# Fourier sums over both halves at once, one Silu, a gate group first, and the context rows moved to the fourth and fifth groups

## The chip, the cores and the metric

The kernel runs on one core of one Trainium2 chip. The metric is the device time of one execution in microseconds. Three timed executions of the kernel before gave 1290.10, 1290.96 and 1291.08 us; the median is 1290.96 us.

## The reference

The reference is one layer of a diffusion block over 512 latent tokens of width 2048, with 256 context tokens. All inputs and outputs are fp32. Cut to what matters here, with `h` the normalised and modulated tokens and `hc` the normalised and modulated context:

```
p   = h @ w_in                       # columns q | k | v | z_a | u_b | z_b | g_a | g_b
q   = rope(rmsnorm(q)) * scale;  k = rope(rmsnorm(k));  kc, vc = hc @ w_in[k | v]
y_a = (attention(q, [k, kc], [v, vc]) * silu(z_a)) @ w_pa
y_b = (real(fft2(u_b over 512 positions and 4 groups of 128 channels)) / 256 * silu(z_b)) @ w_pb
out = rmsnorm(x + gate * ((sigmoid(g_a) * y_a + sigmoid(g_b) * y_b) @ w_out))
```

The Fourier mixing is done as matrix products with tables of cosines and sines. Along the 512 positions, the sums and the differences of the two halves of the tokens give the even and the odd frequencies; along the 128 channels of a group, one table of cosines and one of sines follows. A real input needs 257 frequencies of 512, the others are their mirror images.

## The kernel before

**Arithmetic.** An fp32 matrix is split into a high part, which ACT rounds off (L180), and a low part, which DVE gets by subtraction (L181). A product is then three TensorE passes, high by high (L338), low by high (L339) and high by low (L340); `mm3` issues the three.

**Stages.** The first 144.6 us load the tokens, compute the modulation and project u_b and z_b. The channel stage, to 156.1 us, computes the Fourier mixing: `tokens(g)` (for each of four channel groups) sums over positions into a bank `pb` in two parts, even and odd frequencies, and splits each result into `ah` and `al` (L180, L181); `positions(g)` sums over channels into a bank `pd` (L939, L942), and L944 multiplies the result by 1/256 and by silu(z_b) into `part`; `gate_b(g)` makes silu(z_b) by a Sigmoid on ACT (L949) and a multiplication on DVE (L950).

From 156.1 us on come eight groups of 1024 columns of w_in. Each is seven Strassen products (P1, Q5, P2, Q6, P7, Q3, Q4) of four pieces of 12 matmuls of 512 columns. A product takes 10.9 us, a group 76.2 us: the groups start at 156.1, 234.1, 310.2, 386.4, 463.0 and 539.2 us, and so on. `KINDS` gives their kinds: three "qz" groups (queries and z_a), two "gate" groups, one "kv" group, two "gate" groups. After them come attention, the projection of the branches, and the output.

**What sets the order.** PE runs its instructions in order. Weights come as raw tiles `wr` and `R` by SP's and POOL's queues, are partly summed on DVE (L268, L276), and are split into `whi` and `wlo`, or into `s` where a form of the tokens is split. The instructions of the channel stage on PE stand in the order of the code; elsewhere a scheduler in the framework sets each engine's order when the kernel is built. In the channel stage, splits of the first weight pieces of group 0 are put behind given instructions of `tokens`.

**After a group's product.** A quarter of a "qz" group holds queries: `rotated` (L1208 on ACT, L1210, L1212, L1215, L1216 on DVE, two operations on POOL) normalises and rotates a 128x1024 half of them into the tile `qr`, and two DMAs on ACT's queue (L1230) store it to `qz_d` in device memory. This work of group g runs beside the first products of group g+1. A "gate" half only takes a Sigmoid on ACT (L1183) and a DMA to `g_d`.

**The context.** The tile `qr` has 2048 columns. During the "qz" groups the first 1024 hold the rotated queries and the others the rotary tables. Later the same tile holds the context's forms: `diag` is its first 256 columns, `cparts` its first 1792, `crs` its last 256. Four raw pieces of context ("cn") give the sums of squares; `context_norm` turns them into two diagonal matrices `diag` (L1315, DVE); `context_spread` multiplies `ones` by them on PE (L1320) and copies the result to `crs` (L1321, ACT); four pieces ("cr") then each go through `context_row`, which fills `cparts` and stores it to `cf_d` by a DMA on ACT's queue (L1345). The "kv" group reads `cf_d` back on SP's queue (L216). `context_piece` says beside which weight piece of groups 3 and 4 each is taken, and the list `jobs` holds small tasks, of which one is issued after each piece of a product.

Of the kernel before, what the change touches and what calls it, by code (L numbers as in the profile page):

```python
# [18 lines left out]
P = 128  # L19
D = 2048  # L20
T = 512
# [26 lines left out]
EVEN = 258  # L48
# [16 lines left out]
KINDS = ("qz", "qz", "qz", "gate", "gate", "kv", "gate", "gate")  # L65
# [57 lines left out]
def block_kernel(ctx, tc, xT, ctx_rows, ctx_toks, x, c_row, w_ss, w_gate, vecs, qkg, rope, dft_c, dft_s,  # L123
# [243 lines left out]
    for p in start_pieces():  # L367
        if p[2:5:2] == (KK - 4, 0):
            stream(("dfts", 0), dft_s[:, : 2 * EVEN], 2 * EVEN, 2, "raw")
            stream(("dftc", 0), dft_c, 3 * P, 1, "raw")  # L370
        elif p[2:5:2] == (KK - 4, 4):
            stream(("dfts", 1), dft_s[:, 2 * EVEN :], T, 2, "raw")
        stream(("start", p), w_start[p[0] : p[0] + P * p[1]].rearrange("(p c) -> p c", p=P), p[1], p[2 + 1])
# [146 lines left out]
    fch = ppool.tile([P, 2, 3 * P], F32R, name="fch")  # L520
    fsq = [ppool.tile([P, 2, 2, EVEN], F32R, name="fsq0")]
# [374 lines left out]
    fsq.append(fnp.tile([P, 2, 2, 256], F32R, name="fsq1"))  # L896
# [19 lines left out]
    AH, low = {}, {}  # L916

    def tokens(g):

        ah, al = (fnp.tile([P, 2, 257], F32R, tag=n, bufs=2, name=uid(n)) for n in ("ah", "al"))  # L920
        c = slice(P * g, P * g + P)
        for e in range(2):
            n = fsq[e].shape[-1]
            acc = bank()
            for a in range(2):
                mm3(acc[:, :n], uh[:, a, e, c], ul[:, a, e, c], fsq[e][:, 0, a, :], fsq[e][:, 1, a, :], a == 0, a == 1)
            k = slice(e, 257 - e, 2)
            low[g] = split_from(acc[:, :n].rearrange("p (r f) -> p r f", r=2), ah[:, :, k], al[:, :, k])[1]
        AH[g] = ah, al

    def positions(g):

        ah, al = AH.pop(g)
        acc = bank2()
        steps = [(256 * q, P * (r and 1 + q), (slice(0, 256) if q == 0 else slice(256, 0, -1)), r)
                 for q in range(2) for r in range(2)]
        for n, (o, t, k, r) in enumerate(steps):
            for m, i in enumerate((0, 1)):
                nc.tensor.matmul(acc[:, o : o + 256], fch[:, i, t : t + P], ah[:, r, k], start=n == m == 0, stop=False,  # L939
                                 skip_group_check=True)  # L940
        for n, (o, t, k, r) in enumerate(steps):
            nc.tensor.matmul(acc[:, o : o + 256], fch[:, 0, t : t + P], al[:, r, k], start=False, stop=n == 3,  # L942
                             skip_group_check=True)
        nc.vector.scalar_tensor_tensor(part[:, 4 + g, :], acc, 1.0 / 256.0, part[:, 4 + g, :], op0=ALU.mult, op1=ALU.mult)  # L944

    def gate_b(g):
        z = part[:, 4 + g, :]
        e = fnp.tile([P, T], F32, tag="sil", bufs=1, name=uid("e"))
        nc.scalar.activation(e, z, ACT.Sigmoid)  # L949
        nc.vector.tensor_tensor(z, z, e, op=ALU.mult)  # L950
# [3 lines left out]
    for g in range(4):  # L954
# [265 lines left out]
    def qz_done(half, c, v, t):  # L1220
# [8 lines left out]
        for b in range(2):  # L1229
            nc.scalar.dma_start(qz_d[4 * group.g : 4 * group.g + 4, :, c, 2 * half + b, :].rearrange("h p d -> p h d"),  # L1230
# [73 lines left out]
    def context_squares(i, raw):  # L1304

        nc.scalar.activation(raw, raw, ACT.Square, accum_out=sums[:, i : i + 1])

    def context_norm():

        ss = sums[:, 4:6]  # L1310
        nc.vector.tensor_tensor(ss, sums[:, 0:4:2], sums[:, 1:4:2], op=ALU.add)
# [11 lines left out]
    def context_row(i, raw):  # L1323
# [11 lines left out]
        for j in range(2):  # L1335
            sa, sb = (shift[:, 2 * i + j + 8 * q, 1:2] for q in range(2))
            d = sums[:, 6 + j : 7 + j]
# [731 lines left out]
```

## Time and profile before

| | |
|---|---|
| median of the runs | 1290.96 us |
| the profiled execution's own time | 1290.61 us |
| its span in the profile | 1288.8 us |
| busy share: PE, DVE, ACT, POOL | 99%, 77%, 53%, 13% |
| channel stage, 144.6 to 156.1 us: busy PE, DVE, ACT | 11.50, 11.22, 8.48 us |
| group 0, 156.1 to 234.1 us: busy PE, DVE, ACT | 77.05, 75.57, 42.22 us |
| group 3, 386.4 to 463.0 us: busy PE, DVE, ACT | 76.60, 65.24, 43.44 us |
| mean granted TensorE clock | 0.998 |

The span is the time from the profile's first to its last instruction; 1.8 us of the execution lie outside it. A timeline row has the start, the duration, the engine, the line, the operation and its tiles, and in brackets the idle time before it with what ended that. Matmuls overlap, so that their pitch (start to start) and not their duration says how fast they follow: 0.12 us for 256 or 258 columns, 0.23 us for 512.

### The profile page before, as it was taken

To read this page: it belongs to the slowest core of one execution; us is meant where nothing else is said; L and a number is where in the kernel's file an instruction comes from. 1 tells how busy PE (TensorE), PEld (TensorE's weight loads), DVE (VectorE), ACT (ScalarE), POOL (GpSimd) and SP (SyncE) were. 2 spreads that over 40 slices of the span, in tenths; PEclk is the share of its full clock that TensorE was granted. 3 is DMA by queue.
4 is the path that set the end of the run, shared out by engine and by line. 5 is a ranking of instruction groups with operands and counts; after the bars stand their busy time and mean duration, and the time that the engine had idled before them with its cause. 6 is when DMAs were issued, how large, how long until landed. Compare 5 with 4: busy or idle time off the path is not lost.

```text
span 1288.8 us, 17680 instructions
## 1 busy us (share of the span) xinstructions
PE 1272.9 (99%) x6586; PEld 1047.9 (81%) x6586; DVE 994.7 (77%) x1305; ACT 682.2 (53%) x1073; POOL 170.8 (13%) x222
## 2 busy tenths in 40 slices
PE   8999999999999999999999999999999999999997
PEld 5677887888888888888888888888888888888886
DVE  5767899889779787658587666788898777887677
ACT  5322654645556555444355544666667646464544
POOL 0000011111102011012031010012100211211210
PEclk9999999999999999999999999999999999999999
DMA  9998588888988988977879897578852989998986
GB/s 378 408 369 344 208 216 248 237 218 261 227 302 236 301 269 260 291 197 184 278 207 259 286 249 237 182 245 241 270 178 75 249 244 258 244 211 229 225 200 179
DMA packets 104486, 319.14 MB, mean 248 GB/s; under 512 B 9904, under 2 KB 33072, under 8 KB 100432
## 3 DMA queue, kind: packets, MB, share of 16 engines
q1 hardware_dynamic: 55056, 197.40, 42.3%
q0 software_dynamic: 27024, 98.19, 35.6%
q10 hardware_dynamic: 22320, 22.42, 5.1%
q8 instruction: 51, 0.84, 0.3%
q14 instruction: 35, 0.29, 0.1%
HBM read 283.36 MB, written 34.61 MB: 247 GB/s over the span
## 4 chain that ended last, share of the span: by engine, by line
PE 91%; DVE 3%; DMA 2%; ACT 2%; issue 1%; SPq 0%; ACTq 0%; DVEq 0%
PE banks L338 10%; PE banks L339 10%; PE banks L340 10%; PE x L340 9%; PE x L338 9%; PE x L339 9%; PE y L340 7%; PE y L339 7%; PE y L338 7%; PE banks L1543 2%; PE pd L566 2%; PE pb L338 1%; PE pb L339 1%; PE pb L340 1%; PE pc L338 1%; DMA wa<-in_w_ss 1%
## 5 line engine op out<-in xcount | busy, mean ns | idle before, releaser
L180 ACT ACTIVATE whi<-R 128x1024 fp32r<-128x1024 f32 x138 | 145.6, 1060 | 142.1 <-PE banks L340 55.3
L181 DVE TENSOR_TENSOR wlo<-R,whi 128x1024 fp32r<-128x1024 f32 x138 | 167.9, 1222 | 57.9 <-ACT whi L180 57.6
L181 DVE TENSOR_TENSOR wlo<-wr,whi 128x1024 fp32r<-128x1024 f32 (+1 forms) x122 | 147.2, 1214 | 63.1 <-ACT whi L180 63.1
L180 ACT ACTIVATE whi<-wr 128x1024 fp32r<-128x1024 f32 (+1 forms) x122 | 127.4, 1052 | 127.3 <-PE y L340 44.3
L338 PE MATMUL banks<-whi,s 128*128 128x512 f32 (+1 forms) x400 | 157.8, 394 | 0.9 <-DVE ev L1106 0.9
L339 PE MATMUL banks<-wlo,s 128*128 128x512 f32 (+1 forms) x400 | 155.8, 389 | 0.0
L340 PE MATMUL banks<-whi,s 128*128 128x512 f32 (+1 forms) x400 | 155.8, 389 | 0.0
L338 PE MATMUL x<-whi,s 128*128 128x512 f32 x352 | 137.1, 390 | 0.0
L340 PE MATMUL x<-whi,s 128*128 128x512 f32 x352 | 137.0, 389 | 0.0
L339 PE MATMUL x<-wlo,s 128*128 128x512 f32 x352 | 136.9, 389 | 0.0
L338 PE MATMUL y<-whi,s 128*128 128x512 f32 x316 | 123.1, 389 | 0.2 <-DVE cxe L1266 0.2
L339 PE MATMUL y<-wlo,s 128*128 128x512 f32 x316 | 123.1, 390 | 0.0
L340 PE MATMUL y<-whi,s 128*128 128x512 f32 x316 | 122.8, 389 | 0.0
L291 POOL DMA_DIRECT2D R<-in_w_g x64 | 56.0, 875 | 415.2 <-DVE wlo L181 212.6
L180 ACT ACTIVATE s<-wr 128x512 fp32r<-128x512 f32 (+2 forms) x93 | 60.9, 678 | 68.1 <-DMA wr<-cf_d 24.9
L338 PEld LDWEIGHTS banks<-whi,s 128*128 128x128 f32 x400 | 75.2, 188 | 16.6 <-DVE ev L1106 1.3
L181 DVE TENSOR_TENSOR s<-wr,s 128x512 fp32r<-128x512 f32 (+2 forms) x93 | 66.7, 750 | 28.3 <-ACT s L180 27.5
L340 PEld LDWEIGHTS banks<-whi,s 128*128 128x128 f32 x400 | 75.1, 188 | 15.3
L339 PEld LDWEIGHTS banks<-wlo,s 128*128 128x128 f32 x400 | 75.2, 188 | 13.6 <-DVE wlo L181 0.2
L340 PEld LDWEIGHTS x<-whi,s 128*128 128x128 f32 x352 | 66.1, 188 | 13.8
L339 PEld LDWEIGHTS x<-wlo,s 128*128 128x128 f32 x352 | 66.1, 188 | 13.7
L338 PEld LDWEIGHTS x<-whi,s 128*128 128x128 f32 x352 | 66.1, 188 | 13.6
(322 smaller groups left out, 2803.2 us busy)
## 6 DMA issues: line engine op xcount, KB each, us to landing
wr<-in_w_g SPq DMA_DIRECT2D x128, 512.0 KB, 5.8
R<-in_w_g POOLq DMA_DIRECT2D x64, 512.0 KB, 7.3
wa<-in_w_ss SPq DMA_DIRECT2D x31, 1024.0 KB, 9.7
R<-in_w_g SPq DMA_DIRECT2D x32, 512.0 KB, 6.0
wr<-in_w_gate SPq DMA_DIRECT2D x32, 512.0 KB, 5.1
wr<-in_w_o SPq DMA_DIRECT2D x24, 512.0 KB, 7.5
R<-in_w_o POOLq DMA_DIRECT2D x24, 512.0 KB, 9.2
wr<-in_w_pab SPq DMA_DIRECT2D x20, 512.0 KB, 6.0
```

The costliest lines, as they stand in the source:

```text
L180: first = nc.scalar.activation(hi, src, ACT.Copy)
L181: return first, nc.vector.tensor_tensor(lo, src, hi.bitcast(F32), op=ALU.subtract)
L291: nc.gpsimd.dma_start(chain[e.pc], e.nxt, accum_op=ALU.add)
L338: nc.tensor.matmul(o, ah, bh, start=start, stop=False, skip_group_check=cont)
L339: nc.tensor.matmul(o, ah, bl, start=False, stop=False, skip_group_check=cont)
L340: nc.tensor.matmul(o, al, bh, start=False, stop=stop, skip_group_check=cont)
L566: nc.tensor.matmul(acc[32 * j : 32 * j + 32], c2[:, n, :], w[:, k, :], start=n < 4, stop=n >= KK - 4)
L1543: nc.tensor.transpose(tp[:, k * P : (k + 1) * P], p[:, k * P : (k + 1) * P], ident)
```

## The change

1. In the channel stage the even frequencies become a table of 129 as before, the odd ones too (128 before): both are 258 wide (`FREQ`). `positions` no longer makes the two mirrored halves as separate sums; it computes the cosine sum and the sine sum once for 258 frequencies, in two banks `pd` and `pc`. ACT copies the second into `odd`, and DVE writes the difference (257 columns) and the sum in reversed order (255 columns) to a tile `y`. The factor 1/256 is in the table of channels.
2. `gate_b` is one Silu on ACT. The multiplication of `y` by silu(z_b) stands after the splits of the first weight pieces (L962).
3. The order of the groups is gate, qz, qz, qz, gate, kv, gate, gate; the columns of `w_g` and the index in `qz_d` follow.
4. The pieces of context move: the sums of squares to group 3, pieces 16, 18, 20 and 22 of its 28 (P7 and Q3), the rows to group 4, its pieces 5, 10, 15 and 20. `context_norm` and `context_spread` are appended to the jobs at the start of group 4, with one empty job between them; before, they were appended at the start of group 3 behind twelve empty jobs. Their sums have columns of their own.

```
-KINDS = ("qz", "qz", "qz", "gate", "gate", "kv", "gate", "gate")
+KINDS = ("gate", "qz", "qz", "qz", "gate", "kv", "gate", "gate")
...
+CTX_NORM, CTX_ROWS = (16, 18, 20, 22), (33, 38, 43, 48)
...
-    if n % 2 == 0 and 0 <= n < 8:
-        return "cn", n // 2
-    if n % 7 == 4 and 18 <= n < 46:
-        return "cr", n // 7 - 2
+    if n in CTX_NORM:
+        return "cn", CTX_NORM.index(n)
+    if n in CTX_ROWS:
+        return "cr", CTX_ROWS.index(n)
...
     def positions(g):
 
         ah, al = AH.pop(g)
-        acc = bank2()
-        steps = [(256 * q, P * (r and 1 + q), (slice(0, 256) if q == 0 else slice(256, 0, -1)), r)
-                 for q in range(2) for r in range(2)]
-        for n, (o, t, k, r) in enumerate(steps):
-            for m, i in enumerate((0, 1)):
-                nc.tensor.matmul(acc[:, o : o + 256], fch[:, i, t : t + P], ah[:, r, k], start=n == m == 0, stop=False,
-                                 skip_group_check=True)
-        for n, (o, t, k, r) in enumerate(steps):
-            nc.tensor.matmul(acc[:, o : o + 256], fch[:, 0, t : t + P], al[:, r, k], start=False, stop=n == 3,
-                             skip_group_check=True)
-        nc.vector.scalar_tensor_tensor(part[:, 4 + g, :], acc, 1.0 / 256.0, part[:, 4 + g, :], op0=ALU.mult, op1=ALU.mult)
+        acc = [b()[:, :FREQ] for b in (bank2, bank3)]
+        for r, o in enumerate(acc):
+            t = slice(P * r, P * r + P)
+            mm3(o, fch[:, 0, t], fch[:, 1, t], ah[:, r, :], al[:, r, :], True, True)
+        odd = fnp.tile([P, FREQ], F32, tag="odd", bufs=2, name=uid("odd"))
+        y = mixed[g] = fnp.tile([P, T], F32, tag="y", bufs=4, name=uid("y"))
+        nc.scalar.copy(odd, acc[1])
+        nc.vector.tensor_tensor(y[:, :257], acc[0][:, :257], odd[:, :257], op=ALU.subtract)
+        nc.vector.tensor_tensor(y[:, 257:], acc[0][:, 255:0:-1], odd[:, 255:0:-1], op=ALU.add)
 
     def gate_b(g):
         z = part[:, 4 + g, :]
-        e = fnp.tile([P, T], F32, tag="sil", bufs=1, name=uid("e"))
-        nc.scalar.activation(e, z, ACT.Sigmoid)
-        nc.vector.tensor_tensor(z, z, e, op=ALU.mult)
+        nc.scalar.activation(z, z, ACT.Silu)
...
             for e in ahead[:g]:
                 split_piece(e)
+    for g in range(4):
+        z = part[:, 4 + g, :]
+        nc.vector.tensor_tensor(z, mixed[g], z, op=ALU.mult)
...
-        if g == 3:
-            jobs += [lambda: None] * 12 + [context_norm, lambda: None, lambda: None, context_spread]
+        if g == KV - 1:
+            jobs += [context_norm, lambda: None, context_spread]
```

**What the change moves on the engines.** Lines of the changed kernel are numbered up to three higher (L181 is L184 there, L1216 is L1217, L1315 is L1316, L1320 is L1321, L1230 is L1231).

In the channel stage DVE's order before was this (`al` is a low part of a Fourier sum, `wlo` and `s` those of group 0's weights and tokens, L944 and L950 the multiplications by 1/256 and silu):

```order
L181 TENSOR_TENSOR al_1497<-pb_1498,ah_1496 128x2x129
L950 TENSOR_TENSOR part<-part,e_1578 128x512
L181 TENSOR_TENSOR al_1497<-pb_1507,ah_1496 128x2x128
L181 TENSOR_TENSOR wlo_1575<-R_1340,whi_1574 128x1024
L944 SCALAR_TENSOR_TENSOR part<-pd_1519,part 128x512
L181 TENSOR_TENSOR al_1534<-pb_1535,ah_1533 128x2x129
L181 TENSOR_TENSOR al_1534<-pb_1544,ah_1533 128x2x128
L181 TENSOR_TENSOR wlo_1596<-R_1341,whi_1595 128x1024
L944 SCALAR_TENSOR_TENSOR part<-pd_1560,part 128x512
L268 TENSOR_TENSOR R_1339<-R_1339,wr_1353 128x1024
```

and now is this:

```order
L184 TENSOR_TENSOR al_1528<-pb_1529,ah_1527 128x258
L184 TENSOR_TENSOR wlo_1566<-R_1340,whi_1565 128x1024
L184 TENSOR_TENSOR al_1528<-pb_1538,ah_1527 128x258
L943 TENSOR_TENSOR y_1561<-pd_1552,odd_1560 128x257
L944 TENSOR_TENSOR y_1561<-pd_1552,odd_1560 128x255
L184 TENSOR_TENSOR wlo_1584<-R_1341,whi_1583 128x1024
L943 TENSOR_TENSOR y_1579<-pd_1570,odd_1578 128x257
L944 TENSOR_TENSOR y_1579<-pd_1570,odd_1578 128x255
L962 TENSOR_TENSOR part<-y_1489,part 128x512
L962 TENSOR_TENSOR part<-y_1523,part 128x512
```

The four multiplications by silu(z_b) stand behind the low part of the third weight piece now, and a low part of a weight piece stands between the two last `al`, which the last sum over channels needs.

The spreading of the context's norms on PE stood between the products Q6 and P7 of group 3 (the last rows of Q6 with its bank `y`, the first of P7 with its bank `x`):

```order
L338 MATMUL y_3463<-s_433,s_1869 128x512
L339 MATMUL y_3463<-s_434,s_1869 128x512
L340 MATMUL y_3463<-s_433,s_1870 128x512
L1320 MATMUL y_3705<-qr,ones 128x128 [waits DVE_49] x2
L338 MATMUL x_3712<-s_571,s_1761 128x512 [waits Activation_49]
L339 MATMUL x_3712<-s_572,s_1761 128x512 [waits DVE_49]
L340 MATMUL x_3712<-s_571,s_1762 128x512
```

Now it stands in Q5 of group 4, in the second of its four pieces (the bank of Q5 is `y_3995`):

```order
L341 MATMUL y_3995<-whi_3960,s_1658 128x512
L342 MATMUL y_3995<-wlo_3961,s_1658 128x512
L343 MATMUL y_3995<-whi_3960,s_1659 128x512
L1321 MATMUL y_3977<-qr,ones 128x128 [waits DVE_49,PE_49]
L1321 MATMUL y_3977<-qr,ones 128x128 [waits DVE_49]
```

Before, 192 matmuls of group 3 stood ahead of it; now 69 of group 4 do: 48 of P1, 12 of Q5's first piece, and 9.

The two writes of `diag` on DVE stood among the weight splits of group 3 (`s` and `wlo` are low parts, L276 sums of raw weights):

```order
L181 TENSOR_TENSOR s_287<-R_1342,s_286 128x2x256 [waits DMASW2_49,Activation_49]
L276 TENSOR_TENSOR wr_3569<-R_1339,wr_3569 128x1024 [waits DMAHW1_49]
L181 TENSOR_TENSOR s_434<-R_1342,s_433 128x2x256 [waits Activation_49]
L1315 TENSOR_SCALAR qr<-ident,small 128x128 [waits DMAHW0_49]
L1315 TENSOR_SCALAR qr<-ident,small 128x128
L181 TENSOR_TENSOR s_572<-wr_3569,s_571 128x2x256 [waits Activation_49]
```

and now stand directly behind the last rotation (L1217 is its last step, and its store follows on ACT's queue):

```order
L1216 TENSOR_TENSOR qr<-qr,y_3894 128x1024 [waits DVE_49]
L184 TENSOR_TENSOR s_572<-wr_4014,s_571 128x2x256 [waits DMAHW5_49,Activation_49]
L1217 TENSOR_TENSOR qr<-qr,small 128x1024 [waits DVE_49,Pool_49]
L184 TENSOR_TENSOR s_735<-wr_4014,s_734 128x2x256 [waits PE_49,Activation_49]
L1316 TENSOR_SCALAR qr<-ident,small 128x128 [waits DMAHW1_49,DVE_49]
L1316 TENSOR_SCALAR qr<-ident,small 128x128
L184 TENSOR_TENSOR wlo_4061<-wr_4034,whi_4060 128x1024 [waits DMAHW6_49,Activation_49]
```

The first of the two waits for a DMA (DMAHW1) in the new order: it is the store of the rotated queries from the columns of `qr` that `diag` overwrites. Before, the wait was for the same store (DMAHW0 there), and thirteen instructions of DVE stood between the last rotation (L1216) and L1315.

More of the change, by code (lines that the diff above doesn't have):

```diff
@@ L47 @@
 HL, MORE_HL = 3, 2
-EVEN = 258
+FREQ = 258
 FORMS = ("Z5", "S2", "S3", "S4")
@@ L1229, in qz_done @@
         for b in range(2):
-            nc.scalar.dma_start(qz_d[4 * group.g : 4 * group.g + 4, :, c, 2 * half + b, :].rearrange("h p d -> p h d"),
+            nc.scalar.dma_start(qz_d[4 * group.g - 4 : 4 * group.g, :, c, 2 * half + b, :].rearrange("h p d -> p h d"),
                                 r[:, b])
```

40 lines of the change are left out of this document (20 added, 20 removed).

## The prediction, on record before the result

> **What bounds the kernel now.** I began with the page's engine totals and its chain of waits:
>
> ```profile
> span 1288.8 us, 17680 instructions
> PE 1272.9 (99%) x6586; PEld 1047.9 (81%) x6586; DVE 994.7 (77%) x1305; ACT 682.2 (53%) x1073; POOL 170.8 (13%) x222
> PE 91%; DVE 3%; DMA 2%; ACT 2%; issue 1%; SPq 0%; ACTq 0%; DVEq 0%
> ```
>
> PE is busy 99% of the span and carries 91% of the chain, so a change pays by the matmuls it takes away and costs by the waits it puts between matmuls. The windows by stage tell which engine could make PE wait (columns: start and end, length, then busy time and count of each engine, granted clock, DMA share, GB/s):
>
> ```profile
> 144.60:156.10 11.50, 11.50 (x97) 11.50 (x96) 11.22 (x21) 8.48 (x16) 0.53 (x1) 1.00 0.20 79
> 156.10:234.10 78.00, 77.05 (x339) 62.89 (x338) 75.57 (x88) 42.22 (x63) 10.51 (x13) 1.00 0.80 229
> 310.20:386.40 76.20, 76.20 (x337) 63.07 (x337) 59.41 (x75) 41.80 (x81) 10.76 (x12) 1.00 0.87 251
> 386.40:463.00 76.60, 76.60 (x341) 63.50 (x340) 65.24 (x93) 43.44 (x72) 11.65 (x12) 1.00 0.91 273
> 148.40:212.70 64.30, 63.35 (x309) 52.88 (x307) 64.04 (x80) 36.75 (x60) 11.04 (x14) 1.00 0.73 194
> ```
>
> In the channel stage and most of group 0 DVE (the third engine) has no slack: 64.04 us of 64.30. In groups 2 and 3 it has 17 and 11 us, and PE no gap. Where DVE's fullness reaches PE, its timeline shows in Q3 of group 0:
>
> ```profile
> 156.13 0.40 PE L338 MATMUL x<-whi,s 128*128 128x512 f32 x1
> 209.16 0.50 PE L339 MATMUL x<-s,s 128*128 128x512 f32 x1 [0.71 <-DVE s L181]
> 212.01 0.39 PE L339 MATMUL y<-s,s 128*128 128x512 f32 x1
> 212.64 0.50 PE L340 MATMUL y<-s,s 128*128 128x512 f32 x1 [0.24 <-DVE s L181]
> 234.08 0.39 PE L338 MATMUL x<-whi,s 128*128 128x512 f32 x1
> 310.24 0.39 PE L338 MATMUL x<-whi,s 128*128 128x512 f32 x1
> 386.40 0.39 PE L338 MATMUL x<-s 128*128 128x512 f32 x1
> ```
>
> Group 0 begins at 156.13 and waits twice for low parts of a form. Counted by pitch (0.23 us a matmul) these waits cost 0.87 and 0.40 us. From group 1 on, a group takes 76.16 us without a wait.
>
> **Fourier sums, Silu, multiplication.** A channel group's sums over channels were twelve matmuls of 256 columns:
>
> ```profile
> 147.47 1.12 PE L939 MATMUL pd<-ah,fch 128*128 128x256 f32 x8
> 148.43 0.64 PE L942 MATMUL pd<-al,fch 128*128 128x256 f32 x4
> 148.91 0.28 PE L338 MATMUL pb<-fsq,uh 128*128 128x258 f32 x1
> ```
>
> Eight take 0.96 us and four 0.48: 0.12 each. Now there are six of 258; the sums over positions stay at twelve. PE loses 4 x 6 x 0.12 = **2.9 us**. DVE does not lose work:
>
> ```profile
> 148.53 1.22 DVE L181 TENSOR_TENSOR wlo<-R,whi 128x1024 fp32r<-128x1024 f32 x1
> 149.66 0.69 DVE L944 SCALAR_TENSOR_TENSOR part<-pd,part 128x512 f32<-128x512 f32 x1
> 150.27 0.43 DVE L181 TENSOR_TENSOR al<-pb,ah 128x258 fp32r<-128x258 f32 x1
> 150.62 0.68 DVE L950 TENSOR_TENSOR part<-part,e 128x512 f32<-128x512 f32 x1
> 151.22 0.42 DVE L181 TENSOR_TENSOR al<-pb,ah 128x256 fp32r<-128x256 f32 x1
> ```
>
> Start to start, 1024 columns take 1.13 us, 512 take 0.60, about 257 take 0.33 to 0.35. Taken out: four L944 and four L950, 4.8 us. Put in: eight half-width operations (L943, L944), 2.6 us, and four multiplications (L962), 2.4 us. The net is +0.2 us on a full engine. ACT gets four copies of some 0.4 us (the nearest row is the high part of 258 columns, below, 407 ns) and keeps four activations; with 8.48 us of 11.50 busy it has room. The new DVE order puts one 1024-wide low part ahead of the last `al`, which the last sum over channels needs, so about 0.85 us of PE's 2.9 is lost at once: I place group 0's start at 156.13 - 2.9 + 0.85 = 154.1.
>
> **Gate group first.** What counts then is when DVE has the last low part that Q3 needs. Before, the queries' rotation in group 0 stood ahead of it: two 512-wide operations, four of 256, two of 1024, 4.8 us; a gate group has none (its Sigmoid is ACT's). I add up the new DVE order from the same weight split (148.4) to that low part: 33 of 1024 columns, 32 of 512 and 12 of about 258, 33 x 1.135 + 32 x 0.605 + 12 x 0.335 = 60.8, so 209.3. PE's pure work from group 0's start to that matmul is 212.64 - 156.13 less the waits of 0.87 and 0.40, 55.2; it would come there at 154.1 + 55.2 = 209.3. Both meet; PE gets there at about 209.4 instead of 212.64. **Gain 3.2 us**, with a lower bound of 2 (DVE's waits for tiles take another us) and an upper bound of 4.2 (the 2.9 and the two waits entire).
>
> A second table load appears, since Silu's and Sigmoid's tables both come in group 0 (groups of ACT's instructions; mean ns of one behind the busy time):
>
> ```profile
> L180 ACT ACTIVATE ah<-pb 128x258 fp32r<-128x258 f32 (+1 forms) x8 | 3.3, 407 | 3.0 <-PE pb L340 3.0
> L949 ACT ACT_TABLE_LOAD x1 | 1.3, 1283 | 0.0
> ```
>
> ACT is busy 42.22 us of that group's 78, and the load stands at a gate's Sigmoid, whose result only goes to device memory: I take nothing, at most 1.3 us if a split of weights stands right behind it. The rotations move to the beginnings of groups 2 to 4, where DVE has 11 to 17 us left: nothing.
>
> **The context, the term that decides.** `context_spread` on PE (four small matmuls) keeps its price, only its place changes. Before, it did not wait; these rows are PE's, ACT's queue's, POOL's and DVE's, then the landing of the stores from a view of `qz_d` at three times, each the last row of its view:
>
> ```profile
> 429.92 0.60 PE L1320 MATMUL y<-qr,ones 128*128 128x128 f32 x4
> 249.08 1.41 ACTq L1230 DMA_DIRECT2D qz_d<-qr  x2
> 323.07 0.93 ACTq L1230 DMA_DIRECT2D qz_d<-qr  x2
> 403.60 1.09 ACTq L1230 DMA_DIRECT2D qz_d<-qr  x2
> 400.28 2.00 POOL L1197 TENSOR_TENSOR small<-small,mhalf 128x8 f32<-128x8 f32 x1
> 402.35 1.22 DVE L1216 TENSOR_TENSOR qr<-qr,small 128x1024 f32<-128x1024 f32 x1
> 418.38 0.48 DVE L1315 TENSOR_SCALAR qr<-ident,small 128x128 f32<-128x128 f32 x2
> DMA to landing us min/median/max: 4.7/5.5/6.3
> DMA to landing us min/median/max: 8.6/8.8/9.0
> DMA to landing us min/median/max: 11.8/13.1/14.3
> ```
>
> The last rotated half of a queries' group ends 12.8 to 17.2 us after the next group's start (249.08 - 234.08 = 15.0; 323.07 - 310.24 = 12.8; 403.60 - 386.40 = 17.2) and is then stored from the columns that `diag` overwrites. So `diag` can be written when the first store has landed, 4.7, 8.6 or 11.8 us later. Before, DVE came to `diag` at 418.38, 3.0 us after the landing at 415.4, and PE at 429.92, with 11 us to spare: in group 3, twelve empty jobs stood ahead. Now no such distance is left. By the new PE order 69 matmuls of group 4 stand ahead of the spread: it is reached 69 x 0.227 = **15.6 us** after the group's start. By the new DVE order, from the end of group 3's last product come L1107 (1.1), three low parts (3.4), the rotation (4.8) and three half splits (1.8), 11.1; with the 2.0 us of power on POOL before the last step, partly beside other work, I put L1217's end at 13.7 and the store's issue at 13.8, between the 12.8 and the 15.0 seen. Then: 13.8 + 8.6 (the middle landing) + 0.55 for `diag` = 22.95, against 15.6: **PE stands for 7.3 us**. Best case by these rows: 12.8 + 4.7 + 0.55 - 15.6 = 2.4 us; worst: 17.2 + 11.8 + 0.55 - 15.6 = 14 us. Behind the waiting `diag` on DVE stand weight splits that PE needs some 10 us later by its own clock, which has stopped too, so it is paid once. Group 4's POOL and SP loads go on meanwhile, and nothing later becomes early enough to give PE the time back.
>
> Does the store land sooner? The Trainium skill, "DMA: Bandwidth & Descriptors", section "Anatomy of one DMA — SWDGE (gpsimd) path", gives a transfer's time as 2.0 us fixed plus bytes over 436 GB/s; by that a store of 256 KB takes an estimated 2.6 us, the stall would be 13.8 + 2.6 + 0.55 - 15.6 = 1.3 us and the sum 1288.9. The three landings above are 2 to 4.5 times that, and the same page, section "Queues, rings and completion order", says why that can be: an engine goes round its queue rows, a packet at a time, so a store shares with the loads in flight. The rows decide for the long landing.
>
> **The end of the context.** Rows of context are now 14 us apart rather than 19, all in group 4. The last store to `cf_d` and its first reader before were:
>
> ```profile
> 498.57 0.33 ACTq L1345 DMA_DIRECT2D cf_d<-qr  x1
> 509.15 0.39 SPq L216 DMA_DIRECT2D wr<-cf_d  x1
> DMA to landing us min/median/max: 3.6/7.6/11.6
> ```
>
> The store was issued 40 us ahead of the "kv" group. By the new order it comes some 62 us into group 4, 14 ahead of that group, and the load, with three loads of weights queued behind it on SP, waits for its landing; two splits of that load stand on DVE ahead of the low part for the "kv" group's first piece. Store 3.6 to about 7, load 3.6 or more, splits 2 x 1.1: 9 to 19 us against 14, so 0 to 5 us; I take 0.7, near the low end, since the waiting at the spread moves the loads' other traffic ahead.
>
> **Sum.** The profiled execution took 1290.6 us (span 1288.8 and 1.8 around it), 0.35 under the median. 1290.6 - 3.2 + 7.3 + 0.7 = **1295.4 us**.
>
> **The rivals.**
> - *Short landing* (0.17): the store lands in 2 to 3 us and is issued at 12.8 or little later, so PE stands for 0 to 1.5 us: 1290.6 - 3.2 + 0.7 = 1288, between 1286.5 and 1289. For it: at that moment only ACT's queue stores. Against it: every one of the three alike stores took longer.
> - *Gain and wait cancel* (0.25): landing like the first store's 4.7 us, issue at 13.8: stall 3.4, kv start free, 1290.6 - 3.2 + 3.4 = 1290.8.
> - *The rows of context run late* (within the slower case, 0.10): the spread is late by 10 us or more, each row waits for the landing of the store before, and the "kv" group's first piece waits the full 5 us: 1290.6 - 3.2 + 9 + 4 = 1300.4. It decides once the spread is over 9 us late, because 14 us of lead at the "kv" group are then used up.
> - *No saving in the channel stage* (0.05, spread over the cases): DVE, not PE, ends it, and group 0 keeps its start at 156; then the rotation's removal alone saves the 1.3 us of waits, and all the times above go up by about 2.
>
> **Chances and range.** About 0.2%, 2.6 us, is what a measurement of this kernel can tell from no change: below 1288.4 is faster, above 1293.5 slower. The forecast itself has 0.48; with the late rows and 0.02 from the cancelling case (where the channel stage saves nothing) slower has 0.60. Within is the rest of the cancelling case, 0.23, and 0.02 of the short landing; faster has the other 0.15 of it. The range takes the short landing's upper half and the late rows' middle: 1288.2 to 1300.5; the likeliest case alone would span 1292.5 to 1299.
>
> **What would show it.** Right: in the changed profile L1321 carries an idle time of several us that ends with DVE's L1316, group 4 is that much longer than 76.2 us, and group 0's last wait in Q3 is under 0.5 us with its matmul near 209.4. Wrong on the main term: L1321 without a wait, because the store was issued before 11 us into the group or landed within 2. Wrong on the gain: group 1 starting later than 231.5. Group 5 (kv) should begin with a wait under 1 us; one of several us would be the third rival.

## The result and the profile after

The changed kernel took 1300.33 us (median of six executions, 1298.06 to 1301.78) against 1290.95 us before (six executions in the same sessions, 1290.10 to 1291.18): a ratio of 1.0072, with a 95% interval of 1.0059 to 1.0085. It is slower by 9.4 us. The profiled execution took 1300.45 us, its span is 1298.7 us, 9.9 more than the 1288.8 before.

These are the page's totals of the changed kernel:

```profile
span 1298.7 us, 17647 instructions
PE 1275.0 (98%) x6562; PEld 1046.8 (81%) x6562; DVE 996.5 (77%) x1308; ACT 684.6 (53%) x1077; POOL 167.6 (13%) x222
```

24 matmuls fewer, and yet PE was busy 2.1 us longer: some matmuls got slower. The windows by stage say where (same columns as in the prediction):

```profile
144.60:156.10 11.50, 10.17 (x78) 9.58 (x77) 10.23 (x22) 7.87 (x17) 0.00 (x0) 1.00 0.06 24
156.10:234.10 78.00, 77.55 (x340) 63.35 (x339) 74.14 (x84) 43.85 (x51) 9.10 (x12) 1.00 0.83 248
463.00:539.20 76.20, 70.92 (x299) 57.65 (x299) 56.65 (x98) 38.47 (x67) 8.90 (x10) 0.96 0.78 223
```

In the stretch from 463 us, which lies in group 4, only 299 matmuls ran instead of 337, and the granted clock is 0.96 instead of 1.00. The PE timeline of the changed kernel shows each place; in group 0 and at the ends it reads:

```profile
153.64 0.39 PE L342 MATMUL pd<-al,fch 128*128 128x258 f32 x1 [0.82 <-DVE al L184]
155.02 0.50 PE L341 MATMUL x<-whi,s 128*128 128x512 f32 x1 [0.51 <-ACT odd L942]
211.10 0.50 PE L343 MATMUL y<-s,s 128*128 128x512 f32 x1 [0.34 <-DVE s L184]
461.02 0.39 PE L341 MATMUL x<-whi,s 128*128 128x512 f32 x1
533.14 0.50 PE L342 MATMUL y<-wlo,s 128*128 128x512 f32 x1 [1.47 <-DVE wlo L184]
567.42 0.50 PE L341 MATMUL y<-whi,s 128*128 128x512 f32 x1 [1.01 <-ACT ev L1269]
```

and around the spread in group 4:

```profile
472.60 0.47 PE L341 MATMUL y<-whi,s 128*128 128x512 f32 x1 [0.54 <-DVE qr L1216]
480.91 1.20 PE L1321 MATMUL y<-qr,ones 128*128 128x128 f32 x4 [3.27 <-DVE qr L1316]
481.76 0.77 PE L341 MATMUL y<-whi,s 128*128 128x512 f32 x1
482.33 0.63 PE L342 MATMUL y<-wlo,s 128*128 128x512 f32 x1
482.75 0.63 PE L343 MATMUL y<-whi,s 128*128 128x512 f32 x1
...
486.60 0.63 PE L343 MATMUL y<-whi,s 128*128 128x512 f32 x1
487.02 0.44 PE L341 MATMUL y<-whi,s 128*128 128x512 f32 x1
```

Group 0 starts 1.1 us earlier than before (155.02 against 156.13), its last wait is 1.5 us earlier (211.10 against 212.64), and group 4 starts 2.0 us earlier (461.02 against 463.04; 0.4 of it are the spread's matmuls, which no longer stand ahead). From there the time is lost, counted by pitch: 0.7 us at the start of Q5, 3.4 at the spread, 3.0 in the matmuls behind it, which follow at 0.43 us instead of 0.23, 1.6 in Q3 (at 533.14, in the bank `y`; the texts on record call this place Q4, which begins at 535.80), and 0.4 and 1.2 in the kv group. That makes 10.3; with the 0.4 of the spread itself and less the 2.0 it gives 8.7, and the first matmul behind the eight groups does start at 808.17 instead of 799.42, 8.75 us later. Another 1.1 us is lost in the rest of the kernel, in small waits that also differ between executions.

### The profile page after: what moved, and what is told of

It is laid out like the page before. It is cut to its first block, busy times and chain, and to the rows that moved or that the text cites. A ratio compares the mean times of both kernels' runs of the same rounds, so it can differ in the third digit from the quotient of the medians.

```text
span 1298.7 us, 17647 instructions
## 1 busy us (share of the span) xinstructions
PE 1275.0 (98%) x6562; PEld 1046.8 (81%) x6562; DVE 996.5 (77%) x1308; ACT 684.6 (53%) x1077; POOL 167.6 (13%) x222
## 4 chain that ended last, share of the span: by engine, by line
PE 52%; DVE 1%; ACT 1%; DMA 1%; issue 1%; ACTq 0%
PE banks L341 10%; PE banks L343 9%; PE banks L342 9%; PE y L341 3%; PE y L342 3%; PE y L343 3%; PE x L343 3%; PE x L342 3%; PE x L341 3%; PE banks L1544 2%; DMA s<-yb_d 1%; PE banks L1658 1%; PE banks L1559 0%; DMA wr<-in_w_pab 0%; PE banks L1391 0%
## 5 line engine op out<-in xcount | busy, mean ns | idle before, releaser
L184 DVE TENSOR_TENSOR wlo<-R,whi 128x1024 fp32r<-128x1024 f32 x138 | 167.7, 1220 | 54.9 <-ACT whi L183 54.7
L184 DVE TENSOR_TENSOR wlo<-wr,whi 128x1024 fp32r<-128x1024 f32 (+1 forms) x123 | 148.2, 1212 | 64.2 <-ACT whi L183 63.6
L341 PE MATMUL y<-whi,s 128*128 128x512 f32 x320 | 126.0, 394 | 1.5 <-ACT ev L1269 1.0
L342 PE MATMUL y<-wlo,s 128*128 128x512 f32 x320 | 125.9, 393 | 1.6 <-DVE wlo L184 1.5
L343 PE MATMUL y<-whi,s 128*128 128x512 f32 x320 | 125.4, 392 | 0.0
L184 DVE TENSOR_TENSOR s<-wr,s 128x512 fp32r<-128x512 f32 (+2 forms) x91 | 65.9, 749 | 29.3 <-ACT s L183 28.3
L342 PEld LDWEIGHTS banks<-wlo,s 128*128 128x128 f32 x400 | 75.2, 188 | 13.8 <-DVE wlo L184 0.2
```

Source lines behind the costliest of these rows:

```text
L184: return first, nc.vector.tensor_tensor(lo, src, hi.bitcast(F32), op=ALU.subtract)
L341: nc.tensor.matmul(o, ah, bh, start=start, stop=False, skip_group_check=cont)
L342: nc.tensor.matmul(o, ah, bl, start=False, stop=False, skip_group_check=cont)
L343: nc.tensor.matmul(o, al, bh, start=False, stop=stop, skip_group_check=cont)
```

## Experiments

Ratios are to the kernel before, timed in the same session, with 95% intervals. Spans are of the profiled execution.

### The parts apart

**e1, the Fourier part alone.** The kernel before with the new sums, Silu and the moved multiplication; order of groups and context as before.

> The kernel before with the Fourier sums, the Silu and the later multiplication of the change alone; the order of groups and the context stay as they were. Theory (DVE sets the end of Q3 in group 0, and it still has the queries' rotation there): PE leaves the channel stage about 1.1 us earlier, as in the changed kernel (155.02 against 156.13), and gives it back in group 0's waits for DVE, so 1290.6 to 1291.2. Rival (the matmuls taken away are a gain of their own): 1288 to 1289.5.

Measured: 1294.00 us (1293.08 to 1294.91), ratio 1.0021 [1.0012, 1.0030]. Neither figure: this part alone makes the kernel 3 us slower. PE left the channel stage 0.8 us earlier and then stood in group 0. PE's timeline of e1:

```profile
205.61 0.50 PE L338 MATMUL x<-whi,s 128*128 128x512 f32 x1 [0.86 <-ACT whi L180]
207.84 0.79 PE L339 MATMUL x<-wlo,s 128*128 128x512 f32 x1 [1.73 <-DVE wlo L181]
208.44 0.63 PE L340 MATMUL x<-whi,s 128*128 128x512 f32 x1
```

The same matmul of Q3 that came at 212.64 before comes at 215.92. The windows of DVE show why; first the kernel before, then e1:

```profile
144.60:150.00 5.40, 5.40 (x47) 5.40 (x46) 5.31 (x11) 4.75 (x10) 0.00 (x0) 1.00 0.17 68
```

```profile
144.60:150.00 5.40, 5.40 (x45) 5.32 (x44) 4.14 (x9) 4.70 (x11) 0.00 (x0) 1.00 0.17 68
```

Ahead of 148.5 us ACT's high parts set DVE's pace. With the multiplications out DVE is busy 4.14 us of this window instead of 5.31, and waits four times for `ah`, 1.3 us in all. Three of the four removed multiplications L950 stood there (these are DVE's rows of the kernel before):

```profile
140.39 0.69 DVE L950 TENSOR_TENSOR part<-part,e 128x512 f32<-128x512 f32 x1 [0.34 <-ACT e L949]
145.80 0.69 DVE L950 TENSOR_TENSOR part<-part,e 128x512 f32<-128x512 f32 x1
147.25 0.69 DVE L950 TENSOR_TENSOR part<-part,e 128x512 f32<-128x512 f32 x1
```

Taking them out frees nothing: DVE only waits instead. In the full stretch behind 148.5 us the change takes out five operations of 0.60 us (four L944, one L950) and puts in eight of 0.34 and four of 0.60: +2.1 us. One wait of 1.15 us for a weight's high part at 167.9 and a start 0.2 us later make 3.5 in all, against 3.3 measured at that matmul. (In e1's profiled execution the channel stage itself began 0.3 us later, at 144.86 instead of 144.60.)

**e2, the order alone.** Gate group first and the context moved, the old Fourier sums.

> The kernel before with the gate group first and the context moved, and the old Fourier sums. Theory (nearly all of the loss is in the context's new place): group 0 loses its two waits (1.3 us), the spread waits 3 to 4 us with a slow clock behind it, and the waits at the end of group 4 and in the kv group stay, so 1299 to 1301. Rival (the new sums upset the channel stage or group 0 and make a part of the loss): below 1297.

Measured: 1300.50 us (1298.20 to 1300.98), 1.0068 [1.0051, 1.0084], as the theory said, with a longer wait at the spread than its 3 to 4 us. PE's waits of e2: the time in all, the number, and the longest:

```profile
PE y L1323 <- DVE qr L1318: 4.6, 1, 4.6
PE y L342 <- DVE wlo L184: 1.8, 2, 1.5
PE y L341 <- ACT ev L1271: 1.3, 1, 1.3
PE y L341 <- DVE qr L1218: 0.8, 1, 0.8
```

These are the places of the changed kernel. (Lines of e2 are two higher.) In the profiled execution group 4 started at 462.47, 1.45 us later than with the new sums (0.4 of it was there when the channel stage began), and the spread waited 1.4 us longer. So the new sums bring about 1 us by group 4 when the rotation is out of group 0; but the medians, with ranges of about 3 us each, do not show it: 1300.33 with them, 1300.50 without.

### The spread and PE's clock

**e4, the wait filled with work.** The changed kernel with

```
+        for _ in range(27):
+            nc.tensor.matmul(acc[:, :P], ones, qr[:, 512:640], start=True, stop=True)
         for b in range(2):
             nc.tensor.matmul(acc[:, b * P : b * P + P], ones, diag[:, b, :], start=True, stop=True)
```

> The changed kernel with 27 products of ones and rotated queries on PE directly ahead of the spread (their result is not used), 5.9 us, so that PE works while DVE waits for the store. Theory (an idle time of about 3 us is what halves PE's clock for the next 6.6 us): the granted clock stays at 1.00 through Q5 of group 4, the idle time at the spread is under 1.5 us, and although 5.9 us of work were added the time is that of the changed kernel to within 1.5 us. Rival (the clock falls for another reason, the load or the place): the clock falls to 0.5 here too, and the time is 3 us or more above the changed kernel.

Measured: 1299.58 us (1297.52 to 1304.51), 1.0072 [1.0050, 1.0094]; span 1297.1 us. PE's timeline of e4:

```profile
473.86 6.19 PE L1321 MATMUL y<-qr,ones 128*128 128x128 f32 x54
481.14 0.71 PE L1323 MATMUL y<-qr,ones 128*128 128x128 f32 x4 [1.10 <-DVE qr L1316]
481.61 0.48 PE L343 MATMUL y<-whi,s 128*128 128x512 f32 x1
```

and its granted clock in two windows behind that (in the changed kernel 0.50 from 481 to 487 us):

```profile
482.00:484.00 2.00, 2.00 (x10) 1.62 (x9) 1.71 (x5) 1.32 (x2) 0.00 (x0) 1.00 0.00 0
484.00:486.00 2.00, 2.00 (x10) 1.68 (x9) 2.00 (x5) 1.13 (x3) 0.00 (x0) 1.00 0.43 90
```

The 27 products are 54 matmuls in the profile, of 0.11 us each. These 5.9 us of useless work cost nothing that the times show (the ratio is that of the changed kernel): the clock stays whole, matmuls follow at 0.23 us. The place and the loads are the same, so the idle time is what halves the clock. The wait of 1.6 us in Q3 is also missing in this execution; why is open.

**e3, the diagonals where no store reads.** The changed kernel with

```
-    crs, diag = qr[:, 1792:], qr[:, :256].rearrange("p (b c) -> p b c", b=2)
+    crs, diag = qr[:, 1792:], qr[:, 1792:].rearrange("p (b c) -> p b c", b=2)
```

> The changed kernel with the two diagonal matrices in the last 256 columns of qr, where only rotary tables stand that DVE itself read last, and so without the wait for the store of the queries. Theory A (the spread's wait on PE is the loss there): the idle time of 3.3 us at L1321 and the slow matmuls behind it go, 6 us less than the changed kernel, 1294. Theory B (the store's landing holds whatever comes next in qr): by its order the first row of context (L1332) now waits for the landing on DVE, with a low part of Q5's third piece behind it that PE needs 17 us into the group; PE waits there 3 to 5 us, and the time stays at 1299 to 1301.

Measured: 1296.21 us (1295.56 to 1300.84), 1.0048 [1.0030, 1.0066], 4.1 us under the changed kernel's median. One of its four executions took 1300.84 us, and the two intervals overlap, so the size is uncertain; the profiled spans differ by 4.6 us (1294.1 against 1298.7). The wait at the spread and the slow matmuls behind it are gone. As theory B said, DVE now waits for the landing at the first row of context (DVE's waits between 455 and 545 us):

```profile
DVE qr L1332 <- DMA qz_d<-qr: 5.1, 1, 5.1
DVE qr L1332 <- DMA cf_d<-qr: 2.7, 2, 2.0
```

but PE did not stand in Q5 for it, against theory B. What theory A did not foresee: in Q3 of group 4 PE waited 0.7, 1.0 and 2.4 us, more than the 1.6 of the changed kernel, with a slow clock after the last. So the wait at the spread was a real cost, and part of what it cost came back in Q3, the last product but one before the kv group.

**e6 and e7, the rows later.** Both are e3 with other places for the rows of context; e7 also has the norm two jobs later.

```
-CTX_NORM, CTX_ROWS = (16, 18, 20, 22), (33, 38, 43, 48)
+CTX_NORM, CTX_ROWS = (16, 18, 20, 22), (36, 40, 44, 48)      # e6
+CTX_NORM, CTX_ROWS = (16, 18, 20, 22), (38, 41, 44, 47)      # e7
```

> Run e3 (the diagonal matrices in columns of qr that need no store) with the rows of context at pieces 36, 40, 44 and 48 of the count from group 3, instead of 33, 38, 43 and 48: the first comes three pieces, 8 us, later, the last stays. Theory A (e3's remaining 4.2 us of waits in Q4 come from the last row's work on DVE and its raw tiles at the end of group 4): they stay, 1295.5 to 1297. Theory B (they come from the first row's wait for the store, 5 us in which DVE does nothing and which it carries on to Q4): the wait of L1332 for the store is gone, Q4's waits fall under 2 us, and the time is 1292.5 to 1294.5.

> Run e3 with the norm and the spread two jobs later, and the rows of context at pieces 38, 41, 44 and 47: 8 us apart, the last one piece earlier than in the changed kernel. Theory A of e6 (the last row is what makes Q4 wait): the waits move one piece forward with it and stay within 1.5 us of e3's, 1295 to 1297, or more since rows 8 us apart wait for each other's stores. Theory B: the same 1292.5 to 1294.5 as e6.

Measured: e6 1295.13 us (1293.92 to 1297.24), 1.0032 [1.0018, 1.0047]; e7 1295.24 us (1292.38 to 1297.89), 1.0031 [1.0021, 1.0041]. Theory B's times fall, though its mechanism is half right: in e6 DVE's wait for the store is gone and 1.3 us of waits are left in Q3 (its "Q4"), but 3.3 us came to the kv group. A's times are nearer (e7's median lies in them, e6's 0.4 us under), but its place is not right. ACT's and PE's rows of e6 show what is late:

```profile
559.41 0.63 ACT L183 ACTIVATE s<-wr 128x512 fp32r<-128x512 f32 x1 [5.11 <-DMA wr<-cf_d]
561.37 0.58 ACT L1269 COPY ev<-y 128x512 f32<-128x512 f32 x1
...
562.00 0.79 PE L341 MATMUL y<-whi,s 128*128 128x512 f32 x1 [3.09 <-ACT ev L1269]
```

ACT waits 5.1 us for a piece of the stored context to be read back, and behind that split stands the copy that frees a bank for PE. The times of e7 spread over 5.5 us; its profiled execution was its fastest (1292.38 us), and there the Q3 wait was 1.65 us and the kv wait 0.65. Why it differs so much from one execution to the next was not found.

### Can the context go elsewhere?

**e10 and e11, the kv group one group later.** All parts of the change (e10), and without the new sums (e11), with

```
-KINDS = ("gate", "qz", "qz", "qz", "gate", "kv", "gate", "gate")
-NQZ, KV = 3, 5
+KINDS = ("gate", "qz", "qz", "qz", "gate", "gate", "kv", "gate")
+NQZ, KV = 3, 6
...
-CTX_NORM, CTX_ROWS = (16, 18, 20, 22), (33, 38, 43, 48)
+CTX_NORM, CTX_ROWS = (28, 30, 32, 34), (46, 53, 60, 67)
...
-        if g == KV - 1:
-            jobs += [context_norm, lambda: None, context_spread]
+        if g == 4:
+            jobs += [lambda: None] * 12 + [context_norm, lambda: None, lambda: None, context_spread]
```

> All parts of the changed kernel, but the kv group comes one group later (gate, qz, qz, qz, gate, gate, kv, gate), and the context with its old distances to the last qz group: sums of squares at the first pieces of group 4, twelve empty jobs ahead of the norm, rows 7 pieces apart in groups 4 and 5. Theory (all of the context's loss is that it is squeezed into one group): no wait at the spread, none at the end of the group ahead of kv, none above 0.5 us in kv; what is left is the channel stage and group 0, where the changed kernel was 1.5 us ahead of the kernel before at 212 us and 2 us at group 4: 1288 to 1289.5. Rival (the context costs what it costs wherever it stands behind three qz groups and a gate group): above 1292.

> As e10, with the old Fourier sums and the old multiplication (the order alone). Theory: group 0's two waits (1.3 us) are gone as in e2, and nothing else moves: 1289 to 1290. Against e10 this tells what the new sums are worth when group 0 has DVE to spare: 0.5 to 1 us, since the changed kernel began group 4 at 461.0 and e2 0.4 to 1.3 us later. Rival: e10 is not faster than this by more than 0.2 us.

Measured: e10 1300.40 us (1299.25 to 1300.99), 1.0069 [1.0056, 1.0082]; e11 1300.14 us (1298.01 to 1300.48), 1.0062 [1.0048, 1.0076]. (The entries of the kernel's table `GATE_AT` for the kv group, which place the pieces of w_gate, move with it.) The wait at the spread is gone, as it should be, but my theory falls, and the figures of both rivals came: seven waits of 0.9 to 2.0 us came in the groups behind it, the first one with a slow clock (PE's rows of e10):

```profile
566.61 0.50 PE L342 MATMUL x<-s,s 128*128 128x512 f32 x1 [1.84 <-DVE s L184]
...
568.19 0.63 PE L341 MATMUL x<-s,s 128*128 128x512 f32 x1
```

The other waits are at 692, 701, 702 and 706 us in the kv group and at 773 and 799 us behind it, on splits and copies. The code ties the release of raw tiles to the groups just before and just behind kv (`KV - 1`, `KV + 1`), and these moved with it; which of its rules is to blame these runs do not tell. So no run shows the gate group first with the context placed without a loss. And again the new sums make no difference that the medians show (1300.40 against 1300.14).

### What the Fourier part needs from DVE

**e5 and e8, the multiplications on POOL.** e5 is e1, e8 is e6, each with

```
-        nc.vector.tensor_tensor(z, mixed[g], z, op=ALU.mult)
+        nc.gpsimd.tensor_tensor(z, mixed[g], z, op=ALU.mult)
```

> The Fourier part alone again (run e1), but with the four multiplications by silu(z_b) on POOL instead of DVE, which takes 2.4 us from DVE between the channel stage and Q3 of group 0. Theory (the loss of e1 is DVE being late in group 0, 3.4 us of waits and a slow clock for 3 us behind them): the waits near 206 shrink to below 1 us, the clock stays at 1.00, and the time comes to 1289.5 to 1291.5. Rival (e1's loss is in the order of the weights' loads and splits, not in DVE's work): PE waits 2 us or more there again, 1293 to 1295.

> e6 with the multiplications by silu(z_b) on POOL, as in e5: all four parts of the change, without the waits found so far. Expected by the theory that DVE's 60.8 us to Q3's last low part is the bound of group 0: group 0's wait of 0.5 us and up to 2 us more go, since PE then is the bound there, so 0.5 to 1.5 us less than e6. Rival (group 0 is not bound by DVE with the gate group first): the time of e6 to within 0.4 us.

Measured: e5 1293.53 us (1292.43 to 1295.54), 1.0022 [1.0012, 1.0031]; e8 1297.39 us (1295.47 to 1301.10), 1.0053 [1.0036, 1.0071], 2.3 us more than e6. The time of e5 lies in its rival's range; that of e8 lies outside both figures, though with four executions its interval overlaps e6's. DVE got four instructions fewer, and no time (DVE's, then POOL's rows of e5):

```profile
151.74 2.20 DVE L181 TENSOR_TENSOR wlo<-R,whi 128x1024 fp32r<-128x1024 f32 x1
...
154.86 1.21 DVE L181 TENSOR_TENSOR wlo<-R,whi 128x1024 fp32r<-128x1024 f32 x1
...
156.66 3.91 DVE L268 TENSOR_TENSOR R<-R,wr 128x1024 f32<-128x1024 f32 x2
```

```profile
150.32 2.54 POOL L959 TENSOR_TENSOR part<-y,part 128x512 f32<-128x512 f32 x2 [71.22 <-PE pc L340]
155.10 4.39 POOL L959 TENSOR_TENSOR part<-y,part 128x512 f32<-128x512 f32 x2 [1.36 <-DVE y L941]
```

A DVE split that usually takes 1.2 us took 2.2 when it began beside POOL's multiplication; a pair of sums took 3.9 instead of 2.35 (the pair at 158.69 in e1). That is 1.0 + 1.6 = 2.6 us, more than the 2.4 taken off DVE. The split at 154.86 kept its 1.21 us: it had begun when POOL's second pair started, and that pair took 4.39 us instead of 2.54. In e8, as in e5, the channel stage's wait for `al` grew to 1.8 us, and in e8 the clock fell behind it, at 156.4 us; group 0's own wait in Q3 had gone, as expected.

**e9, the multiplications at once.** e1 with each multiplication directly behind L943 and L944 of its group.

> The Fourier part alone (run e1), with each multiplication by silu(z_b) directly behind its channel group's sums instead of behind the weight splits; a low part of a weight piece then no longer stands between the last two al. Theory (the moved multiplications are what makes DVE late: in the channel stage DVE has idle times in which the multiplications of the kernel before fell, now they fall in the full stretch behind it): PE's wait of 1 us for al goes, the waits in group 0 fall to 1 to 2 us without a slow clock, 1290 to 1292. Rival (it is the DVE work as a whole): as e1, 1293 to 1295.

Measured: 1293.96 us (1292.86 to 1294.59), 1.0021 [1.0012, 1.0030]. As e1, though the clock stayed at 1.00; the rival's figure was right. The place of the multiplications in the stretch does not matter. That their presence in it does is the count of e1; no run takes them off DVE without slowing it by something else.

**e12, Silu alone.** The kernel before with one Silu on ACT and without L950.

```
-        e = fnp.tile([P, T], F32, tag="sil", bufs=1, name=uid("e"))
-        nc.scalar.activation(e, z, ACT.Sigmoid)
-        nc.vector.tensor_tensor(z, z, e, op=ALU.mult)
+        nc.scalar.activation(z, z, ACT.Silu)
```

> The kernel before with one Silu on ACT in place of Sigmoid and the multiplication L950, and nothing else of the change. Theory (only work in DVE's full stretch from 148.4 us to Q3 of group 0 counts: three of the four L950 stand ahead of it, at 140.4, 145.8 and 147.3, in time that DVE would else wait; one stands in it): DVE comes to Q3 0.6 us earlier, the two waits of 0.87 and 0.40 us shrink by about that, 1290.0 to 1290.5, which this measurement can hardly tell from the kernel before. Rival (all 2.4 us of the four count): the waits are gone, 1289.4.

Measured: 1289.48 us (1289.19 to 1290.00), 0.9987 [0.9978, 0.9996]: faster than both kernels. In group 0 one of the two waits is unchanged (PE's row of e12):

```profile
212.21 0.50 PE L340 MATMUL y<-s,s 128*128 128x512 f32 x1 [0.24 <-DVE s L181]
```

By pitch the wait of 0.87 is down to 0.28, the one of 0.40 stays: the theory's 0.6 us of DVE. The median is nearer to the rival's figure, though. The profiled span is only 0.7 us shorter (1288.1); this execution began the channel stage 0.4 us later (145.01 against 144.60). The rest of the 1.5 us by which the medians differ is not explained.

## Why the prediction was right, and where its terms were not

The forecast (slower, 1295.4, within 1288.2 to 1300.5) had the direction and the deciding place. The time fell 0.2 us inside the upper end of the range. In the terms of its sum the trace has -1.6 us up to group 4 (the 2.0 us less the spread's own 0.4) where it had -3.2, +7.1 at the spread where it had +7.3, +3.2 for the end of the context where it had +0.7, and 1.1 us behind the groups that no term had. So the direction was right by its mechanism; that the largest term came within 0.2 us was in part luck. Step by step:

- **Fourier sums and gate group first: 3.2 us of gain predicted, 1.5 measured at Q3.** The wait for `al` in the channel stage, reckoned at 0.85 us, cost 1.05 by pitch (0.82 of it idle). PE then also waited 0.51 us (0.67 by pitch) for ACT's copy of `odd`, where the prediction said that ACT "has room", so group 0 started at 155.0 and not at 154.1. The count of DVE's work was right: 61.0 us from its first weight split (148.42) to the end of the low part that Q3 needs, against 60.8. What was left out of the sum is DVE's one wait in that stretch, for a high part from ACT, which had itself waited 2.9 us for raw weights (DVE's row of the changed kernel):

```profile
167.99 1.23 DVE L184 TENSOR_TENSOR wlo<-R,whi 128x1024 fp32r<-128x1024 f32 x1 [1.59 <-ACT whi L183]
```

- **"The net is +0.2 us on a full engine"** was wrong as well, though the sum of 60.8 does not use it. It took all eight removed DVE operations as taken from the full stretch; three of the four L950 stood ahead of it. e1 shows that term by itself: +2.1 us of DVE work where I had +0.2. The second table load came at the gate's Sigmoid (187.67 us) and PE did not wait behind it, as reckoned. (Of the two old waits of group 0, the one at 209.16 is at the end of P7, in the bank `x`, and not in Q3.)
- **Lower bound of 2 us for that gain:** broken too, by 0.5; it had allowed 1 us for DVE's waits. Group 1 started at 232.54, past the 231.5 named as the sign that the gain was wrong. e2 (the order without the new sums) was only 0.6 us early at group 4, of which 0.4 are the moved spread, so most of the gain came with the sums; in the medians it does not show.
- **The spread: 7.3 us predicted, 7.1 measured (0.7 + 3.4 + 3.0), for reasons half of which I did not have.** The step "PE stands for 7.3 us" failed in size: the store was issued 13.2 us into the group (474.22), close to my 13.8, and landed after 6.2 us, between the 4.7 and the 8.6 of the rows; PE came to the spread 0.9 us later than reckoned, since Q5 had waited 0.7 us for a bank which the rotation still held (L1216). So PE stood 3.3 us. What I left out filled the gap: after standing, PE ran at half its clock for 6.2 us. These are the issue of the store and DVE's waiting for it in the changed kernel:

```profile
474.22 1.38 ACTq L1231 DMA_DIRECT2D qz_d<-qr  x2
...
480.47 0.48 DVE L1316 TENSOR_SCALAR qr<-ident,small 128x128 f32<-128x128 f32 x2 [5.68 <-DMA qz_d<-qr]
```

- **The Trainium skill's sum for the store, 2.6 us and a stall of 1.3, does not hold here:** the landing was 6.2 us. (The section named is on GpSimd's path; this store is issued on ACT's queue. With that stall the forecast's own terms add up to 1289.4, not 1288.9.) The rows show when it would hold. Of the first stores of each pair to `qz_d` in the two kernels, the nine beside which the DMA engines had a busy share of 0.61 to 0.76 landed after 2.3 to 2.6 us; the fifteen beside a share of 0.99 to 1.06 took 3.0 to 11.8. The store of `diag`'s columns is of the second kind (1.04). The Trainium skill's page "TensorE: Matmul & The Clock Gate", Part 1, states that an idle time of about 3.4 us halves the clock until the array has been busy as long again. The trace agrees in kind (0.50 for 6.8 us around 3.3 us of idle time), other runs needed less idle time (last section), and I should have set the rule beside the 7.3 us: by the profile of before alone it could not be seen, since behind the first 20 us PE never stood longer than 0.9 us there.
- **The weight splits behind the waiting `diag`, "so it is paid once":** held; no second wait came in Q5.
- **The end of the context: 0.7 us predicted, 3.2 measured (1.6 in Q3, 0.4 and 1.2 in kv), within its 0 to 5.** The choice near the low end was wrong. Of the two mechanisms named, the read-back at the start of the kv group showed as ACT's waits for `cf_d` (9.0 us in three from 536 to 575 us, against 4.6 in two before), which hold up copies behind them; the wait in Q3, where the last row's DVE work (from 528.2 to 531.9 us) stands directly ahead of the low part that PE needs, I did not name.
- **The rivals.** Short landing: wrong, 6.2 us. Gain and wait cancel: the stall was indeed 3.4 us, as that case had it, but the slow clock and the kv group made it the slower case. Late rows: its time, 1300.4, is what came, but not its mechanism: it decided "once the spread is over 9 us late", and the spread was 3.3 us late; of its 4 us at the kv group's first piece 0.4 were seen in that product. No saving in the channel stage: not as named (PE left it 1.1 us earlier), though the medians with and without the new sums, 1300.33 and 1300.50, are alike.

Settled: the loss comes with the order of the groups and the context's place (e2, without the new sums, has all of it, 1300.50); the spread's wait is a part of it (3 to 4 us less in e3), and the slow clock comes from the idle time (e4). By the trace the places of loss are the context's; no run moves the gate group without the context. Open: why the waits ahead of and in the kv group vary between executions, and which rule makes e10 wait in seven places.

## What to carry to other kernels

Before counting an operation taken off a saturated engine as gain, look at when it ran: one that stood in a gap frees nothing, and its replacement in the full stretch costs its whole time. When a tile is reused behind a store, the wait is the store's landing under load, so leave the distance, or reuse columns that no store reads. A wait on TensorE of about 2 us can cost more than its length, because the matmuls behind it may run at half the clock for 3.4 or 6.8 us (they did in the three runs with a wait above 3 us).

## What the runs showed of the hardware

- **The clock falls by the idle time within a fixed stretch of 3.41 us, not by the length of a wait.** It fell to 0.50 after one wait of 1.84 us (e10), and not after one of 2.54 (e8):

```profile
563.50 0.50 PE L341 MATMUL y<-whi,s 128*128 128x512 f32 x1 [2.54 <-ACT ev L1269]
```

It fell after 1.82 and 0.51 us in the channel stage of e8, and not after the same two waits in e5. The granted clock over time settles this. In each of the 14 traces all switches lie a whole number of 3.41 us apart (in the changed kernel 137 times 3.41 from 12.65 to 480.27 us), as if on a fixed grid. Cut into the stretches of this grid, the traces from 25 to 1280 us agree on one rule. In nine stretches PE was idle for 1.85 us or more, and in the next one the clock was 0.50: 1.85 (e10), 1.87 (e8), 1.88 (e5), 2.26 (e11), 2.27 (e3), 2.34 (e1), 2.63 (changed kernel), 2.97 (e6) and 3.41 (e2). In all others at full clock PE was idle for 1.66 us or less, and the clock held. The 2.54 us of e8 straddle a border and leave 1.66 in one stretch. The clock stayed down for one stretch, or for two where PE still stood for 0.63 us (changed kernel) or 1.20 us (e2) in the first; with 0.25 us (e1) it was one. That cost 1.6 to 3 us. The grid lies differently in every trace, so by this rule the same waits can cost differently from one execution to the next.
- **POOL's two-input multiplications and DVE's hold each other up.** 512 columns took POOL 1.3 to 2.2 us each, and a DVE split that began beside them took 2.20 instead of 1.21 us (e5). The Trainium skill's "SBUF — State Buffer", section "Who interferes with whom", states that a DVE instruction with two inputs in SBUF and a GpSimd instruction that reads SBUF contend; these rows agree.
- **The same store of 256 KB landed after 4.7, 6.2, 8.6 and 11.8 us** at four comparable places, each in the second product of a group, while the DMA engines' busy share was 1.04 to 1.06. The share alone does not tell which of these times it will be.
